# A two-layer hybrid attention step on one core: a new order of the attention parts, norm sums that add squares before the one-column product, and value products issued for two key tiles at a time

## The chip, the core and the metric

The kernel runs on one core of a Trainium2 chip. Its engines are TensorE (PE, with its weight loads shown apart as PEld), VectorE (DVE), ScalarE (ACT), GpSimd (POOL) and SyncE (SP), which issues nearly all transfers. The metric is the device time of one launch in microseconds; lower is better.

## What is computed

One inference step of a backbone of two layers (DEPTH = 2), in fp32, on 128 context tokens and 512 latent tokens of width 1024. Cut to one layer and to the latent tokens (the context tokens pass through the same layer with a conditioning vector of their own and attend to context alone):

```python
sh1, sc1, g1, sh2, sc2, g2 = jnp.split(jax.nn.silu(cvec) @ w_ada + b_ada, 6, axis=-1)
h = rmsnorm(x, norm1_g) * (1 + sc1) + sh1
da_q, da_k, da_v, sw_q, sw_k, sw_v, q_a, kv_a = jnp.split(h @ w_in, offs, axis=-1)
da_o  = diff_attention(q1, q2, [cache | k1], [cache | k2], dv, lam)     # 4 heads, softmax(1) - lam * softmax(2)
sw_o  = swa_latent_attention(q, k, v, cache_k, cache_v, sink)           # 8 heads, 2 key heads, window 128
mla_o = gqa_attention(q, [cache_k | k], [cache_v | v])                  # 4 heads, keys and values from a latent
mix = concat([rmsnorm(da_o, diff_subln_g) * (1 - lam_init), sw_o, mla_o])
x = x + g1 * (mix @ w_out)
h2 = rmsnorm(x, norm2_g) * (1 + sc2) + sh2
x = x + g2 * (square(relu(h2 @ w_up)) @ w_down)                         # 4096 hidden columns
```

`rmsnorm(x) = x * rsqrt(mean(x * x) + EPS) * g`; a last one stands behind the two layers. The keys and values of the context tokens are outputs too.

## The kernel before

**Data.** Activations are kept transposed: `xT` is [128, 8, 640], the eight 128-column chunks of the width on the partitions and the 640 tokens along the free axis. Tokens are handled in two halves, `HALVES = [(0, 256), (256, 640)]`, that is two and three tiles of 128 (`TILES`). A product in fp32 is made of three passes over split operands (`mm3`): high by high, high by low, low by high. So each weight block that arrives (`wr`) is split in `wh` (a rounding copy, on ACT or DVE) and `wl` (a subtraction, on DVE or GpSimd).

**Order.** Everything but the middle of the MLP is recorded as tasks of a planner (`Plan`): an engine or a choice of engines ("A" ACT, "V" DVE, "G" GpSimd, "P" PE), a modelled duration, what it reads and writes, which buffers of which ring it takes (`RINGS`: how many buffers each ring has), and a priority, lower first. `Plan.run` plays the tasks against the modelled durations and so fixes one order for each engine; the instructions are then emitted in that order, and an engine never leaves it. Transfers follow each other in SP's queue in the same way.

**Stages of a layer.** (1) Squares and sums for the first norm, its root, the modulated activations `h` (`emit_h`). (2) The input projection. (3) The attention: the sequence of parts `seq` in the table `KP`, one for each layer. A token `cN` is N conditionings (two chunks of a section of `w_ada`: a load, products `pa`, an `asb` copy, a transpose, `ada`; they supply shifts, scales and gates needed later, those of the next layer's first norm among them). `s0`, `s1` are quads (groups of two heads by two query tiles) of the windowed attention, `d0`, `d1` of the differential and `m0`, `m1` of the latent one. `D`, `V`, `M` prepare queries, keys and values, `wN` is part N of the output product. The place of a token gives the priority of its tasks; `lead`, `prep`, `tr` and `evict` shift kinds of them, and the other entries choose engines (`weights`, `caches`, `keys`, `da`, `out`, `scale`). (4) The output stage: last part of the output product, residual updates (`emit_resid`, a scaled addition to `xT` on DVE), sums for the second norm, its root for each half, `h2`, and the first up products of the MLP (`first_up`). (5) The big product stage of the MLP, in a list `blocks` of up ("u") and down ("d") products written out in order. (6) The last down products (`last_down`), with the sums for the next norm.

**The norm's sums** (`stat`): for each chunk and half, ACT squares `xT` into a buffer `sq` of ring "E" (four buffers), and PE multiplies each 128-token tile of it by a column of ones, which adds the 128 partitions; the eight chunks add up in PSUM (`st`). This happens at five places: at the start, in the output stage of either layer, between the layers, at the end. The root (`rstd`) is a chain of small steps on DVE (`rsq`), a broadcast copy `yb` and transposes on PE into `rb`. In the plan `emit_h` for the second half of the tokens stands `half` (in priority) behind that of the first, with `k` from 0 to 7 as the step of one chunk.

**A quad**: scores into PSUM (`sps`), row maximum on DVE, exponential on ACT (`quad`), the scaling of each row by one over its sum (`scale`, L981 on ACT, L983 on DVE), then for each key tile transposes into PSUM (`pt`, L1095), a copy `PT` to SBUF by ACT or DVE, and the value products (L1099): two heads side by side, 64 output columns of the array each, over up to 256 queries, added up over the key tiles in `O`. Ring "PT" has three buffers.

Of the kernel before, what the change touches and what calls it, by code (L numbers as in the profile page):

```python
# [15 lines left out]
ALU = mybir.AluOpType  # L16
# [11 lines left out]
HALVES = [(0, 256), (256, 640)]  # L28
# [14 lines left out]
N_CST = 900  # L43


RINGS = {"E": 4, "X": 5, "PT": 3, "B": 8, "h": 4, "mix": 3, "quad": 2, "QK": 4, "hs": 2, "wr": 3, "wh": 4, "wl": 4, "zin": 2, "sq4": 2,
         "stt": 10, "osb": 1, "Kc": 1, "ds": 2, "sm": 4, "rsq": 3, "Vsw": 1, "Vda": 1, "Vml": 1, "ckT": 1, "kz": 1,
         "s": 2, "t": 3, "o": 1, "z": 4, "T": 2, "ws": 2}

# [7 lines left out]
DMA0, DMAR = 2.0, 300e3  # L57
WINDOW = 3.413
N_PRE = 2

KP = [
    {"weights": ("A", "V"), "caches": ("A", "V"), "keys": ("AV", "V"), "da": ("AV", "V"), "out": ("AV", "V"),
     "scale": "AV", "lead": 5, "prep": 1000000.0, "tr": 1000000.0, "up": ("A", "V"), "up_prio": 3500000.0,
     "evict": 500000.0, "resid": (4, 4, 8, 8), "half": 0.5,
# [15 lines left out]
def tV(n):  # L82
    return 0.07 + n / 960
# [281 lines left out]
def tile_hybrid_step(ctx: ExitStack, tc: tile.TileContext, i, o):  # L365
    nc = tc.nc
    V, S, G, T = nc.vector, nc.scalar, nc.gpsimd, nc.tensor
# [22 lines left out]
    def add(*a, **k):  # L390
        return cur[0].add(*a, **k)
# [43 lines left out]
    def sl(t, table, key):  # L435
# [11 lines left out]
    ones = sl(cst, CST, "ones")  # L447
# [18 lines left out]
                    in1=sil[:, 2].rearrange("p (k s) -> p k s", s=2), op=ALU.mult)  # L466
# [162 lines left out]
    def open_stats(ring, after=()):  # L629
        if ring == "s":  # L630
            x = mk(ring, [P, 2, 512], F32, "st")
            add("V", 0.1, lambda: V.memset(x.t[:, :, 0:4], 0.0), alloc=[x], prio=0.0, after=after)
            return [(x, lambda a, b, hf=hf: x.t[:, hf, a:b]) for hf in range(2)]
# [3 lines left out]
        return [(x, lambda a, b, x=x: x.t[:, a:b]) for x in st]  # L637

    def stat(st, k, hf, prio):

        a, b = HALVES[hf]
        w = b - a
        n = TILES[hf][1] - TILES[hf][0]
        x, view = st[hf]
        sq = mk("E", [P, NT], F32, "sq")
        add("A", tA(w) + 0.05, lambda: S.activation(out=sq.t[:, 0:w], in_=xT[:, k, a:b], func=AF.Square),
            r=[("x", (k, hf))], alloc=[sq], prio=prio)

        def mm():
            for t in range(n):  # L650
                T.matmul(out=view(t, t + 1), lhsT=sq.t[:, t * P:(t + 1) * P], rhs=ones,  # L651
                         start=False, stop=(k == KD - 1), skip_group_check=True)

        add("P", 0.115 * n, mm, r=[sq], w=[(x, hf)], prio=min(prio, 0.9e6))
# [331 lines left out]
    def quad(l, kind, u, hd, vt, vcols, mix, kt_mix, pr_, hs, at):  # L986
# [9 lines left out]
        for y in range(2):  # L996
            for x in range(2):
                n = 2 * pr_ + y
                h = hd[x]
                q = slice(P + n * P, 2 * P + n * P)  # L1000
                st = mk("stt", [P, 8])
                e2 = mk("E", [P, NT], F32, "e2") if kind == "da" else None
                if kind == "sw":
                    a, tiles = SWT[n]
                    w = len(tiles) * P
                    we = w + 1
                else:
                    w = we = NT
                for j in range(2 if kind == "da" else 1):
# [20 lines left out]
                    else:  # L1030
# [54 lines left out]
        ns = len(slots)  # L1085
        O = mk("o", [P, 256], F32, "O")
        p_t = PAR["tr"] + at
        for z, (kt, have) in enumerate(slots):
            pt, PT = mk("t", [P, 2, 256], F32, "pt"), mk("PT", [P, 2, 256], F32, "PT")
            c, w = have[0] * P, len(have) * P  # L1090

            def tr(pt=pt, kt=kt, have=have):
                for x in range(2):
                    for y in have:
                        T.transpose(pt.t[:, x, y * P:(y + 1) * P], e_.t[:, x, y, pos[y][kt]:pos[y][kt] + P], ident)  # L1095

            def pv(z=z, kt=kt, c=c, w=w, PT=PT):
                for x in range(2):
                    T.matmul(out=O.t[64 * x:64 * x + 64, c:c + w], lhsT=vt.t[:, kt, vcols[x]:vcols[x] + 64],  # L1099
                             rhs=PT.t[:, x, c:c + w], start=(z == 0), stop=(z == ns - 1))  # L1100
# [477 lines left out]
    for l in range(DEPTH + 1):  # L1578
# [134 lines left out]
        with ExitStack() as es:  # L1713
# [108 lines left out]
            for b_, blk in enumerate(blocks):  # L1822
# [182 lines left out]
```

## Time and profile before

| | |
|---|---|
| time, three runs | 1755.74, 1760.19 and 1761.95 us; median 1760.19 |
| the profiled execution | 1761.53 us, of it 1759.8 us from the first instruction to the last (span) |
| PE | 1676.2 us busy (95%), 11335 products |
| DVE | 1242.9 us (71%) |
| ACT | 809.5 us (46%) |
| POOL | 199.5 us (11%) |
| transfers | 163.24 MB, 93 GB/s in the mean |

A row of a group reads: line, engine, operation, written and read buffers, partitions by elements and type, count, then busy us and mean ns of one, then the engine's idle time just before these instructions with what ended it. A row of a time table reads: window in us from the start, its length, then busy us and count of PE, PEld, DVE, ACT and POOL, the clock that TensorE was granted (1.00 is full), the share of the DMA engines and GB/s. A row of a timeline reads: start, duration, engine, line, operation, buffers, and in brackets the wait before it and what ended it. "x400" beside the norm's sums counts two passes of PE for each fp32 product of the code.

### The profile page before, as it was taken

The numbers are of one execution on the slowest core, as the hardware profiler recorded it, in microseconds if no ns is written. First come the engines' busy times: TensorE is split into PE (matmuls) and PEld (weight loads), VectorE is DVE, ScalarE is ACT, GpSimd is POOL, SyncE is SP. The second block draws the span as 40 slices with busy tenths as digits, with TensorE's granted clock in tenths as the row PEclk, the third lists the DMA queues.
The fourth block names the chain that finished last, engine by engine and source line by source line (L and its number), as shares of the span: only waits on it lengthen the run. The fifth ranks groups of instructions, "written<-read, shape, count | busy, mean of one in ns | idle before, by whom it ended". The sixth has DMA issues, their size and how long they took to land.

```text
span 1759.8 us, 29841 instructions
## 1 busy us (share of the span) xinstructions
PE 1676.2 (95%) x11335; PEld 1487.5 (85%) x11335; DVE 1242.9 (71%) x3229; ACT 809.5 (46%) x1798; POOL 199.5 (11%) x165
## 2 busy tenths in 40 slices
PE   7899999899899999999999999989889999999997
PEld 6687567568799999999998865857779999999997
DVE  3865778986868667766576767988577867766654
ACT  3532667774525333333254347777353433333321
POOL 0000001100013222212000000300001322212200
PEclk9999999999899999999999999999999999999999
DMA  9322553340122122222213244231111222222121
GB/s 314 102 84 87 200 165 96 108 139 25 61 70 87 61 87 82 97 85 77 89 52 98 88 135 137 90 108 56 36 61 50 71 93 76 96 88 70 61 73 61
DMA packets 67391, 163.24 MB, mean 93 GB/s; under 512 B 6896, under 2 KB 31280, under 8 KB 67248
## 3 DMA queue, kind: packets, MB, share of 16 engines
q1 hardware_dynamic: 67248, 161.34, 28.3%
q8 instruction: 90, 1.47, 0.3%
q14 instruction: 53, 0.43, 0.1%
HBM read 153.15 MB, written 8.16 MB: 92 GB/s over the span
## 4 chain that ended last, share of the span: by engine, by line
PE 79%; DVE 10%; ACT 4%; DMA 2%; issue 1%; POOL 1%; SPq 0%; DVEq 0%; ACTq 0%; POOLq 0%
PE pu L1853 18%; PE pu L543 8%; PE pu L542 8%; PE pu L544 8%; PE pt L1095 3%; PE O L1099 3%; PE po L542 3%; PE po L544 3%; PE pz L830 3%; PE pz L832 3%; PE po L543 3%; PE pz L831 3%; PE sps L1026 2%; PE st L651 2%; DMA zin<-zda 2%
## 5 line engine op out<-in xcount | busy, mean ns | idle before, releaser
L407 DVE TENSOR_TENSOR wl<-wr,wh 128x512 fp32r<-128x512 f32 (+2 forms) x290 | 287.0, 1010 | 62.0 <-ACT wh L414 37.4
L399 ACT ACTIVATE wh<-wr 128x512 fp32r<-128x512 f32 (+1 forms) x228 | 161.0, 736 | 282.6 <-PE pu L543 176.3
L542 PE MATMUL pu<-Gt,wh 128*128 128x384 f32 (+1 forms) x896 | 277.7, 310 | 5.1 <-DVE r L1449 5.1
L543 PE MATMUL pu<-Gt,wh 128*128 128x384 f32 (+1 forms) x896 | 277.6, 310 | 0.0
L544 PE MATMUL pu<-Gt,wl 128*128 128x384 f32 (+1 forms) x896 | 277.6, 310 | 0.0
L735 DVE SCALAR_TENSOR_TENSOR xT<-pu,ada,xT 128x128 f32<-128x128 f32 x336 | 134.8, 434 | 146.0 <-PE pu L544 145.7
L542 PEld LDWEIGHTS pu<-Gt,wh 128*128 128x128 f32 x896 | 170.6, 190 | 5.7 <-DVE r L1449 5.7
L543 PEld LDWEIGHTS pu<-Gt,wh 128*128 128x128 f32 x896 | 170.6, 190 | 0.0
L544 PEld LDWEIGHTS pu<-Gt,wl 128*128 128x128 f32 x896 | 170.5, 190 | 0.0
L1853 PE MATMUL pu<-Tl,wh 128*128 128x320 f32 x448 | 138.0, 308 | 0.0
L1853 PE MATMUL pu<-Th,wl 128*128 128x320 f32 x448 | 138.0, 308 | 0.0
L1853 PE MATMUL pu<-Th,wh 128*128 128x320 f32 x448 | 138.0, 308 | 0.0
L830 PE MATMUL pz<-wh,hh 128*128 128x512 f32 (+1 forms) x320 | 128.3, 401 | 2.1 <-DVE m L763 1.0
L831 PE MATMUL pz<-wl,hh 128*128 128x512 f32 (+1 forms) x320 | 123.4, 386 | 2.6 <-DVE wl L407 2.6
L735 DVE SCALAR_TENSOR_TENSOR xT<-po,ada,xT 128x128 f32<-128x128 f32 (+1 forms) x192 | 77.0, 434 | 66.3 <-PE po L544 65.2
L832 PE MATMUL pz<-wh,hl 128*128 128x512 f32 (+1 forms) x320 | 123.7, 386 | 0.1
L1048 DVE TENSOR_REDUCE stt<-sps 128x1 f32<-128x640 f32 (+2 forms) x160 | 116.1, 737 | 9.1 <-PE sps L1041 5.0
L1853 PE MATMUL pu<-hh,wh 128*128 128x320 f32 x336 | 104.2, 310 | 4.6 <-DVE r L1868 4.6
L1056 ACT ACTIVATE quad<-sps,stt 128x640 f32<-128x640 f32 (+2 forms) x128 | 91.2, 713 | 27.5 <-DVE stt L1048 26.9
L1853 PE MATMUL pu<-hh,wl 128*128 128x320 f32 x336 | 103.8, 309 | 0.0
L1853 PE MATMUL pu<-hl,wh 128*128 128x320 f32 x336 | 103.6, 308 | 0.0
L1427 POOL TENSOR_TENSOR xT<-xT,tm 128x256 f32<-128x256 f32 (+1 forms) x32 | 30.1, 941 | 619.8 <-ACT tm L1423 365.3
(313 smaller groups left out, 3930.7 us busy)
## 6 DMA issues: line engine op xcount, KB each, us to landing
wr<-in_w_ada SPq DMA_DIRECT2D x80, 512.0 KB, 3.8
wr<-in_w_up SPq DMA_DIRECT2D x64, 512.0 KB, 3.5
wr<-in_w_down SPq DMA_DIRECT2D x64, 512.0 KB, 3.5
wr<-in_w_in SPq DMA_DIRECT2D x24, 512.0 KB, 3.5
wr<-in_w_out SPq DMA_DIRECT2D x16, 512.0 KB, 4.5
wq<-in_w_ada SPq DMA_DIRECT2D x6, 1024.0 KB, 6.9
wr<-in_w_in SPq DMA_DIRECT2D x8, 416.0 KB, 3.4
xT<-in_xT SPq DMA_DIRECT2D x4, 640.0 KB, 7.1
```

The lines of the kernel that those rows point to most:

```text
L399: S.activation(out=out, in_=in_, func=AF.Copy)
L407: eng.tensor_tensor(out=out, in0=a, in1=b, op=ALU.subtract)
L542: T.matmul(out=out, lhsT=w[0], rhs=a[0], start=first, stop=False)
L543: T.matmul(out=out, lhsT=w[0], rhs=a[1], start=False, stop=False)
L544: T.matmul(out=out, lhsT=w[1], rhs=a[0], start=False, stop=last)
L735: V.scalar_tensor_tensor(out=xT[:, m, a:b], in0=po[:, a - a0:b - a0], scalar=ada[l][:, sec, m, s:s + 1], in1=xT[:, m, a:b], op0=ALU.mult, ...
L830: T.matmul(out=out, lhsT=h_at(h, "h", k, tk), rhs=wh[:, x], start=(k == 0), stop=False)
L831: T.matmul(out=out, lhsT=h_at(h, "h", k, tk), rhs=wl[:, x], start=False, stop=False)
L832: T.matmul(out=out, lhsT=h_at(h, "l", k, tk), rhs=wh[:, x], start=False, stop=(k == KD - 1))
L1048: add("V", tV(we) - 0.01, lambda st=st, j=j, view=view: V.tensor_reduce(out=st.t[:, j:j + 1], in_=view(), axis=AX.X if kind == "sw" else A ...
L1056: S.activation(out=out, in_=view(), func=AF.Exp, bias=st.t[:, j:j + 1], accum_out=st.t[:, 4 + j:5 + j])
L1853: T.matmul(out=out, lhsT=w_[:, k], rhs=a_[:, k], start=new and k == 0 and y == 0, stop=k == 3 and y == 2, skip_group_check=True)
```

## The change

Four things, in one edit.

1. `stat` adds the squares of chunks 0 to 6 on DVE into the first one's buffer, which stays taken for that time; PE multiplies this sum by ones when chunk 6 is in, and the square of chunk 7 by itself. So 10 one-column products at each of the five places, where there were 40.
2. `N_PV = 2`: in a quad the value products of two key tiles are one task, behind both copies `PT`; a last odd tile goes alone. Ring "PT" has four buffers.
3. `KP` has new entries for both layers: the sequence with conditionings one by one between the quads, other priorities (`lead`, `prep`, `tr`, `evict`, `half`) and other engines.
4. In the big product stage a down block covers both 128-column pieces (`mi`) of one half of the tokens, where it covered both halves of one piece. The products are the same.

```diff
-RINGS = {"E": 4, "X": 5, "PT": 3, ...
+RINGS = {"E": 4, "X": 5, "PT": 4, ...
...
+N_PV = 2
...
 KP = [
-    {"weights": ("A", "V"), "caches": ("A", "V"), "keys": ("AV", "V"), "da": ("AV", "V"), "out": ("AV", "V"),
-     "scale": "AV", "lead": 5, "prep": 1000000.0, "tr": 1000000.0, ...
-     "evict": 500000.0, "resid": (4, 4, 8, 8), "half": 0.5,
-     "seq": "c2 c1 c1 c2 s0 s0 s0 c2 c2 s0 c2 c1 w0 s1 c2 s1 D0 s1 s1 ..."
+    {"weights": ("A", "V"), "caches": ("AV", "V"), "keys": ("A", "V"), "da": ("AV", "V"), "out": ("AV", "V"), "scale": "AV",
+     "lead": 40, "prep": 1000000.0, "tr": 900000.0, ... "evict": 1000000.0,
+     "resid": (4, 4, 8, 8), "half": 3.0,
+     "seq": "c1 c1 c1 c1 s0 s0 c1 c1 s0 c1 c1 c1 c1 s0 s1 c1 s1 D0 s1 s1 c1 w0 ..."
...
-    {"weights": ("A", "V"), "caches": ("AV", "VG"), "keys": ("AV", "V"), "da": ("AV", "V"),
-     "out": ("AV", "V"), "scale": "AV", "lead": 30, "prep": 950000.0, "tr": 900000.0, ...
-     "split": "V", "evict": 999995.0, "resid": (4, 4, 8, 8), "half": 0.5, ...
+    {"weights": ("AV", "V"), "caches": ("A", "V"), "keys": ("A", "V"), "da": ("A", "V"), "out": ("AV", "V"), "scale": "A",
+     "lead": 30, "prep": 1000000.0, "tr": 900000.0, ... "evict": 1000000.0,
+     "resid": (4, 4, 8, 8), "half": 8.5, ...
...
 def stat(st, k, hf, prio):
-        x, view = st[hf]
+        x, view, part = st[hf]
         sq = mk("E", [P, NT], F32, "sq")
         add("A", tA(w) + 0.05, lambda: S.activation(out=sq.t[:, 0:w], in_=xT[:, k, a:b], func=AF.Square),
             r=[("x", (k, hf))], alloc=[sq], prio=prio)
+        if k == 0:
+            part.append(sq)
+        elif k < KD - 1:
+            acc = part[0]
+            add("V", tV(w), lambda: V.tensor_tensor(out=acc.t[:, 0:w], in0=acc.t[:, 0:w], in1=sq.t[:, 0:w], op=ALU.add),
+                r=[sq], w=[acc], prio=prio)
+        if k < KD - 2:
+            return
+        src = part[0] if k < KD - 1 else sq
 
         def mm():
             for t in range(n):
-                T.matmul(out=view(t, t + 1), lhsT=sq.t[:, t * P:(t + 1) * P], rhs=ones,
+                T.matmul(out=view(t, t + 1), lhsT=src.t[:, t * P:(t + 1) * P], rhs=ones,
                          start=False, stop=(k == KD - 1), skip_group_check=True)
...
 def quad(...):
-        for z, (kt, have) in enumerate(slots):
+        z0, pvs = 0, []
+        for kt, have in slots:
...
-            add("P", 0.255 * len(have), pv, r=[PT, (vt, kt)], ... prio=p_t, narrow=True)
+            pvs.append((kt, c, w, PT))
+            if len(pvs) < N_PV and kt != slots[-1][0]:
+                continue
...
+            add("P", 0.255 * sum(w // P for _, _, w, _ in pvs), pv,
+                r=[q for kt, _, _, PT in pvs for q in (PT, (vt, kt))], ... prio=p_t, narrow=True)
+            z0, pvs = z0 + len(pvs), []
...
-                        blocks.extend(("d", g, mc, mi, len(tiles)) for mi in range(2))
+                        blocks.extend(("d", g, mc, hf, len(tiles)) for hf in range(2))
...
-                    for hf in range(2):
-                        a0, b0 = HALVES[hf]
+                    for mi in range(2):
+                        m = mc * 2 + mi
+                        mm_ = slice(mi * P, (mi + 1) * P)
```

What the edit moves shows in the engines' orders. PE at the start: `st` are the norm's sums, `pa` the first conditionings (whose transposes write `pt`), `rb` the transposed root of a half. Before:

```order
L651 MATMUL st<-cst,sq 128x1 x37
L576 MATMUL pa<-wq,sc 32x128 x8
L651 MATMUL st<-cst,sq 128x1 x3
L581 MATMUL pt<-cst,asb 128x128
L576 MATMUL pa<-wq,sc 32x128 x8
L581 MATMUL pt<-cst,asb 128x128
L669 MATMUL rb<-cst,yb 128x128 x5
```

After:

```order
L663 MATMUL st<-cst,sq 128x1 x10
L578 MATMUL pa<-wq,sc 32x128 x16
L681 MATMUL rb<-cst,yb 128x128 x2
L583 MATMUL pt<-cst,asb 128x128 x2
L578 MATMUL pa<-wq,sc 32x128 x8
L681 MATMUL rb<-cst,yb 128x128 x3
```

The 40 products of the sums are 10, and the root's transposes of the first half (two) stand ahead of the last conditioning, those of the second half (three) behind it. PE in the first layer's windowed attention, from one quad's transposes (L1095) to the next part: `O` are value products of the latent tokens, `Oc` those of the context. Before:

```order
L1095 MATMUL pt<-cst,quad 128x128 x4
L1215 MATMUL Oc<-PTc,Vsw 64x128 x2
L1095 MATMUL pt<-cst,quad 128x128 x8
L1099 MATMUL O<-PT,Vsw 64x256 x2
L576 MATMUL pa<-wr,sc 32x256 x4
L1099 MATMUL O<-PT,Vsw 64x256 x2
L1265 MATMUL pt<-cst,sq_2625 128x128 x4
L1099 MATMUL O<-PT,Vsw 64x256 x2
L1099 MATMUL O<-PT,Vsw 64x128 x2
L1265 MATMUL pt<-cst,sq_2642 128x128 x4
```

After:

```order
L1108 MATMUL pt<-cst,quad 128x128 x8
L583 MATMUL pt<-cst,asb 128x128 x2
L1108 MATMUL pt<-cst,quad 128x128 x4
L578 MATMUL pa<-wr,sc 32x256 x4
L1122 MATMUL O<-PT,Vsw 64x256 x6
L1122 MATMUL O<-PT,Vsw 64x128 x2
L1285 MATMUL pt<-cst,sq_2333 128x128 x4
L1285 MATMUL pt<-cst,sq_2338 128x128 x4
```

The value products of a quad stood in four pieces between other work; the new order has those of two key tiles, and here of all four, next to each other, behind all the transposes. DVE in the second layer's output stage, where the residual updates of the second half of the tokens (128x384) meet the root and the `h2` work of the first half (128x256; `hs`, `hh`, `hl`). Before:

```order
L719 TENSOR_TENSOR hs<-xT,rb 128x256
L407 TENSOR_TENSOR hl_14617<-hs,hh_14615 128x256
L719 TENSOR_TENSOR hs<-xT,rb 128x256 x2
L585 TENSOR_REDUCE ada_93<-pt 128x4
L587 TENSOR_TENSOR ada_93<-ada_93,cols 128x4
L407 TENSOR_TENSOR hl_14617<-hs,hh_14615 128x256
L401 CAST hh_14615<-hs 128x256
L735 SCALAR_TENSOR_TENSOR xT<-po,ada_93,xT 128x384
L407 TENSOR_TENSOR hl_14617<-hs,hh_14615 128x256
L735 SCALAR_TENSOR_TENSOR xT<-po,ada_93,xT 128x384
```

After:

```order
L747 SCALAR_TENSOR_TENSOR xT<-po,ada_93,xT 128x384
L655 TENSOR_TENSOR sq<-sq 128x384
L747 SCALAR_TENSOR_TENSOR xT<-po,ada_93,xT 128x384
L655 TENSOR_TENSOR sq<-sq 128x384
L623 TENSOR_TENSOR rsq<-rsq 128x2
L747 SCALAR_TENSOR_TENSOR xT<-po,ada_93,xT 128x384
L655 TENSOR_TENSOR sq<-sq 128x384
L624 SCALAR_TENSOR_TENSOR rsq<-rsq 128x2
L409 TENSOR_TENSOR wl<-wr,wh 128x1024
L625 SCALAR_TENSOR_TENSOR rsq<-rsq 128x2
L613 TENSOR_SCALAR rsq<-st 128x3
```

The last updates of the second half stood within the `h2` work of the first half, behind its root; now they all stand ahead of the end of that root, each with an addition of squares (L655) behind it.

More of the change, by code (lines that the diff above doesn't have):

```diff
@@ L43 @@
 N_CST = 900
-RINGS = {"E": 4, "X": 5, "PT": 3, "B": 8, "h": 4, "mix": 3, "quad": 2, "QK": 4, "hs": 2, "wr": 3, "wh": 4, "wl": 4, "zin": 2, "sq4": 2,
+RINGS = {"E": 4, "X": 5, "PT": 4, "B": 8, "h": 4, "mix": 3, "quad": 2, "QK": 4, "hs": 2, "wr": 3, "wh": 4, "wl": 4, "zin": 2, "sq4": 2,
          "stt": 10, "osb": 1, "Kc": 1, "ds": 2, "sm": 4, "rsq": 3, "Vsw": 1, "Vda": 1, "Vml": 1, "ckT": 1, "kz": 1,
@@ L59 @@
 N_PRE = 2
+N_PV = 2
 KP = [
-    {"weights": ("A", "V"), "caches": ("A", "V"), "keys": ("AV", "V"), "da": ("AV", "V"), "out": ("AV", "V"),
-     "scale": "AV", "lead": 5, "prep": 1000000.0, "tr": 1000000.0, "up": ("A", "V"), "up_prio": 3500000.0,
-     "evict": 500000.0, "resid": (4, 4, 8, 8), "half": 0.5,
[4 rows of a table removed]
-     "up_prio": 3500000.0, "split": "V", "evict": 999995.0, "resid": (4, 4, 8, 8), "half": 0.5,
-     "seq": "s1 s0 c1 c2 s1 c1 s1 s1 c1 D0 c1 s0 c1 c1 c1 s0 s0 w1 c1 "
-            "w0 d0 c1 D1 V0 c1 c1 c1 d0 d1 M0 d1 c1 w2 m0 m0 M1 m1 m1"},
+    {"weights": ("A", "V"), "caches": ("AV", "V"), "keys": ("A", "V"), "da": ("AV", "V"), "out": ("AV", "V"), "scale": "AV",
+     "lead": 40, "prep": 1000000.0, "tr": 900000.0, "up": ("A", "V"), "up_prio": 3500000.0, "evict": 1000000.0,
+     "resid": (4, 4, 8, 8), "half": 3.0,
+     "seq": "c1 c1 c1 c1 s0 s0 c1 c1 s0 c1 c1 c1 c1 s0 s1 c1 s1 D0 s1 s1 c1 w0 "
+            "c1 w1 c1 d0 c1 c1 V0 c1 c1 c1 D1 c1 d1 d0 c1 d1 M0 c1 m0 m0 c1 w2 "
+            "M1 m1 m1"},
+    {"weights": ("AV", "V"), "caches": ("A", "V"), "keys": ("A", "V"), "da": ("A", "V"), "out": ("AV", "V"), "scale": "A",
+     "lead": 30, "prep": 1000000.0, "tr": 900000.0, "up": ("A", "V"), "up_prio": 3500000.0, "evict": 1000000.0,
+     "resid": (4, 4, 8, 8), "half": 8.5,
+     "seq": "c1 s0 s1 s1 c1 c1 c1 s1 s1 D0 c1 s0 c1 c1 c1 s0 w1 s0 w0 c1 c1 c1 "
+            "d0 V0 D1 d0 c1 c1 c1 c1 d1 M0 d1 m0 m0 M1 w2 m1 m1"},
 ]
@@ L632, in open_stats @@
             add("V", 0.1, lambda: V.memset(x.t[:, :, 0:4], 0.0), alloc=[x], prio=0.0, after=after)
-            return [(x, lambda a, b, hf=hf: x.t[:, hf, a:b]) for hf in range(2)]
+            return [(x, lambda a, b, hf=hf: x.t[:, hf, a:b], []) for hf in range(2)]
         st = [mk(ring, [P, 512], F32, "st") for _ in range(2)]
@@ L636, in open_stats @@
             add("V", 0.1, lambda x=x: V.memset(x.t[:, 0:4], 0.0), alloc=[x], prio=0.0, after=after)
-        return [(x, lambda a, b, x=x: x.t[:, a:b]) for x in st]
+        return [(x, lambda a, b, x=x: x.t[:, a:b], []) for x in st]
     def stat(st, k, hf, prio):
@@ L647, in stat @@
             r=[("x", (k, hf))], alloc=[sq], prio=prio)
+        if k == 0:
[7 more added lines that the diff above has]
+        src = part[0] if k < KD - 1 else sq
         def mm():
             for t in range(n):
[L651 removed]
+                T.matmul(out=view(t, t + 1), lhsT=src.t[:, t * P:(t + 1) * P], rhs=ones,
                          start=False, stop=(k == KD - 1), skip_group_check=True)
[L654 removed]
+        add("P", 0.115 * n, mm, r=[src], w=[(x, hf)], prio=min(prio, 0.9e6))
     def rstd(st, hf, rb, prio):
@@ L1095, in tr @@
                         T.transpose(pt.t[:, x, y * P:(y + 1) * P], e_.t[:, x, y, pos[y][kt]:pos[y][kt] + P], ident)
[L1097 to L1100, printed above, removed]
             add("P", 0.22 * len(have), tr, r=[(e_, (x, y)) for x in range(2) for y in have],
@@ L1106, in quad, with pv @@
                 r=[pt], alloc=[PT], prio=PAR["evict"] + at)
-            add("P", 0.255 * len(have), pv, r=[PT, (vt, kt)], w=[] if z == 0 else [O], alloc=[O] if z == 0 else [], prio=p_t,
-                narrow=True)
+            pvs.append((kt, c, w, PT))
+            if len(pvs) < N_PV and kt != slots[-1][0]:
+                continue
+            def pv(pvs=pvs, z0=z0, O=O):
+                for z, (kt, c, w, PT) in enumerate(pvs):
+                    for x in range(2):
+                        T.matmul(out=O.t[64 * x:64 * x + 64, c:c + w], lhsT=vt.t[:, kt, vcols[x]:vcols[x] + 64],
+                                 rhs=PT.t[:, x, c:c + w], start=(z0 + z == 0), stop=(z0 + z == ns - 1))
+            add("P", 0.255 * sum(w // P for _, _, w, _ in pvs), pv,
+                r=[q for kt, _, _, PT in pvs for q in (PT, (vt, kt))], w=[] if z0 == 0 else [O],
+                alloc=[O] if z0 == 0 else [], prio=p_t, narrow=True)
+            z0, pvs = z0 + len(pvs), []
         c0 = P + pr_ * 256
@@ L1826, in tile_hybrid_step @@
                 if kind == "d":
-                    g, mc, mi = f, q, x
-                    m = mc * 2 + mi
-                    mm_ = slice(mi * P, (mi + 1) * P)
+                    g, mc, hf = f, q, x
+                    a0, b0 = HALVES[hf]
                     whv, wlv = (z.rearrange("p (k n) -> p k n", k=4) for z in (wh, wl))
-                    for hf in range(2):
-                        a0, b0 = HALVES[hf]
+                    for mi in range(2):
+                        m = mc * 2 + mi
+                        mm_ = slice(mi * P, (mi + 1) * P)
                         pu = bank()
```

3 rows, old and new, of the table KP are left out of this document.

## Prediction

> **What bounds the kernel now.** I read the page first: span, busy time by engine, the chain that ended last by engine.
>
> ```profile
> span 1759.8 us, 29841 instructions
> PE 1676.2 (95%) x11335; PEld 1487.5 (85%) x11335; DVE 1242.9 (71%) x3229; ACT 809.5 (46%) x1798; POOL 199.5 (11%) x165
> PE 79%; DVE 10%; ACT 4%; DMA 2%; issue 1%; POOL 1%; SPq 0%; DVEq 0%; ACTq 0%; POOLq 0%
> ```
>
> PE ends the program: work taken off it counts unless another engine is about as full in that stage. So I cut the span where PE goes from one stage to the next. The rows are the start, the first attention, the output stage (output product, norm, first up products), the big product stage, the last down products, the second attention, the second output stage; the columns are busy us of PE, PEld, DVE, ACT, POOL, then the granted clock.
>
> ```profile
> 0.00:34.00 34.00, 24.38 (x153) 21.25 (x154) 9.24 (x47) 12.89 (x28) 0.20 (x4) 1.00 0.96 327
> 173.00:419.00 246.00, 231.04 (x1811) 159.93 (x1811) 194.91 (x547) 172.76 (x428) 17.46 (x24) 0.99 0.42 132
> 419.00:524.00 105.00, 93.74 (x609) 89.59 (x609) 72.61 (x165) 41.13 (x80) 8.04 (x6) 0.93 0.15 51
> 524.00:868.00 344.00, 341.99 (x2334) 341.46 (x2333) 239.04 (x418) 124.36 (x232) 74.44 (x50) 1.00 0.25 85
> 868.00:904.00 36.00, 36.00 (x267) 36.00 (x265) 22.61 (x66) 17.40 (x39) 0.00 (x0) 1.00 0.13 38
> 1026.00:1267.00 241.00, 225.03 (x1707) 163.87 (x1705) 198.15 (x543) 165.56 (x416) 17.12 (x25) 0.98 0.32 100
> 1267.00:1367.00 100.00, 88.75 (x569) 84.57 (x568) 70.81 (x159) 39.72 (x76) 8.07 (x6) 0.93 0.16 53
> ```
>
> The big product stage (524 to 868) and the last down products have no room but less PE work. The attentions are full on PE (94%) with DVE at 79 and 82%: there a PE saving may turn into a wait. The output stages are where PE is least busy.
>
> **Part 1: squares summed first.** 200 one-column products become 50; the trace shows each as two passes (400 in all), so 300 passes go. 60 DVE additions come: 30 of 256 columns, 30 of 384. Their price from the same form on DVE, and that of a pass from a place where nothing waits, the last down products:
>
> ```profile
> L651 PE MATMUL st<-cst,sq 128*128 128x1 f32 x400 | 57.0, 261 | 8.0 <-ACT sq L646 8.0
> L407 DVE TENSOR_TENSOR hl<-hs,hh 128x256 fp32r<-128x256 f32 x16 | 6.5, 420 | 0.0
> L407 DVE TENSOR_TENSOR hl<-hs,hh 128x384 fp32r<-128x384 f32 x8 | 4.4, 551 | 0.0
> 879.89 0.50 PE L651 MATMUL st<-cst,sq 128*128 128x1 f32 x4
> 881.65 0.28 PE L544 MATMUL po<-Gt,wl 128*128 128x256 f32 x1
> 881.77 0.50 PE L651 MATMUL st<-cst,sq 128*128 128x1 f32 x4
> 881.97 0.61 DVE L735 SCALAR_TENSOR_TENSOR xT<-po,ada,xT 128x128 f32<-128x128 f32 x2 [1.27 <-PE po L544]
> ```
>
> One round (12 products, 4 passes) takes 881.77 - 879.89 = 1.88 us; a product starts 0.12 us after the last (881.77 - 881.65), so the passes take 1.88 - 12 x 0.12 = 0.44, or 0.11 each. 300 x 0.11 = 33 us of PE work at full clock, 6.6 in each of five places; the additions are 30 x 0.42 + 30 x 0.55 = 29 us of DVE. What a place yields depends on who waits.
>
> Last down products, both layers: DVE idles 1.27 us per round and now adds 0.42, so it stays ahead. Between the layers 6.5. At the end DVE also writes the result, so 5.5; bounds 4 and 6.6 each.
>
> Start: these passes run at half speed and hold up the squares.
>
> ```profile
> 7.58 15.95 PE L651 MATMUL st<-cst,sq 128*128 128x1 f32 x74 [7.58 <-ACT sq L646]
> 9.97 0.52 ACT L646 ACTIVATE sq<-xT 128x384 f32<-128x384 f32 x1 [0.77 <-PE st L651]
> 23.56 0.16 DVE L611 TENSOR_SCALAR rsq<-st 128x2 f32<-128x2 f32 x1 [19.55 <-PE st L651]
> 66.77 0.50 PE L830 MATMUL pz<-wh,hh 128*128 128x512 f32 x1 [0.92 <-DVE hh L401]
> 69.84 0.80 PE L831 MATMUL pz<-wl,hh 128*128 128x512 f32 x1 [2.57 <-DVE wl L407]
> ```
>
> 15.95 / 74 = 0.215 us a pass; ACT waits for the buffers they read, and DVE idles 19.55 us until the sum is there. After: two of four buffers are pinned as sums, so a round of both halves is two squares and two additions in turn, at least 0.42 + 0.55 = 0.97 on DVE and about 1.15 with the hand-overs. Eight from 7.1 end near 16; the first half's seven products of two passes then take 3 us at most at 0.215, partly beside the last squares, so the root starts near 17.5, not 23.56. DVE then makes h until the waits at 66.77 and 69.84, both for DVE, so the gain runs through the projection: 6. Bounds 3.5 (the loads, busy 96% here, end last) and 7.
>
> The Trainium skill speaks against that term. TensorE: Matmul & The Clock Gate, "Part 1: The HAM clock gate (the "warmup" mystery)", says that the half clock is released after about 3.4 us of sustained products. By that rule the passes after 11 us would take 0.11, the old chain would end near 18 and the start would gain nothing: 1725 in place of the 1719 below. The row shows 0.215 held for 16 us, so the measurement decides.
>
> The first output stage in pieces, and two forms of DVE there (a split of a weight block, a residual update):
>
> ```profile
> 418.00:425.00 7.00, 7.00 (x57) 6.48 (x57) 2.86 (x9) 1.94 (x5) 0.00 (x0) 1.00 0.00 0
> 425.00:432.00 7.00, 4.70 (x32) 4.03 (x31) 3.28 (x10) 0.42 (x1) 0.00 (x0) 1.00 0.01 2
> 432.00:440.00 8.00, 8.00 (x56) 8.00 (x56) 4.67 (x14) 2.95 (x6) 0.00 (x0) 1.00 0.00 0
> 440.00:447.00 7.00, 7.00 (x52) 7.00 (x51) 4.50 (x14) 3.20 (x6) 0.00 (x0) 1.00 0.23 75
> 447.00:455.00 8.00, 7.71 (x61) 5.91 (x61) 6.98 (x23) 6.92 (x19) 0.00 (x0) 1.00 0.38 133
> 455.00:463.00 8.00, 8.00 (x69) 8.00 (x68) 7.98 (x20) 3.02 (x5) 0.00 (x0) 1.00 0.39 131
> 463.00:474.00 11.00, 4.86 (x19) 3.51 (x18) 8.31 (x23) 6.54 (x15) 0.00 (x0) 0.73 0.01 2
> 474.00:495.00 21.00, 18.46 (x97) 18.14 (x97) 17.62 (x25) 10.71 (x19) 0.00 (x0) 0.90 0.07 24
> ...
> L407 DVE TENSOR_TENSOR wl<-wr,wh 128x1024 fp32r<-128x1024 f32 x112 | 144.3, 1292 | 51.7 <-ACT wh L414 34.1 <-ACT wh L399 17.4
> L735 DVE SCALAR_TENSOR_TENSOR xT<-po,ada,xT 128x384 f32<-128x384 f32 x64 | 39.4, 616 | 39.5 <-PE po L544 39.0
> ```
>
> Output stages up to the norm's first half: DVE is busy 15.3 of 29 us there (418 to 447, four rows), PE 26.7. After, PE loses the 6.6, but DVE gains 5.8 of additions, two late residual updates (0.62 each) and one or two splits of weights (1.3 each) that stood behind: about 24. So DVE is the bound, some 24 for 29: I take 4 in each layer, 8 in all; bounds +3 (the additions delay the updates) and -13 (all of PE's).
>
> **Part 2: the first up products.** From 447 to 495 DVE is busy 40.9 of 48 us; PE stands idle 6 of 11 us around 468, for the second half's root, and falls to half clock. In the new order the second half's updates all stand ahead of the first half's h, and its transposed root comes after 63 (first layer) and 27 (second) of the 96 up products, not after them. DVE's work here shrinks by what moved ahead, 1.2 + 1.3 to 2.6 + some root steps of 0.16, to about 37, plus hand-overs 39; from 46 (448 to the first down product at 494.3) that is 7 a layer, 14 in all. Bounds 4 (DVE waits anyway) and 18 (PE's idle and half clock of both layers gone).
>
> **Part 3: value products by twos, four buffers.** The order has 49 and 43 visits to these narrow products in the attentions before, 28 and 28 after: 36 fewer for the same 288 products.
>
> ```profile
> 414.34 0.65 PE L1099 MATMUL O<-PT,Vml 128*64 128x256 f32 x4
> 414.92 0.66 PE L1095 MATMUL pt<-cst,quad 128*128 128x128 f32 x4
> 341.19 1.45 PE O L1099 x12
> 363.89 1.01 PE O L1099 x8
> ...
> L399 ACT ACTIVATE PT<-pt 128x512 f32<-128x512 f32 x82 | 47.7, 596 | 29.2 <-PE pt L1095 26.8 <-PE O L1099 1.6
> L401 DVE COPY PT<-pt 128x512 f32<-128x512 f32 x46 | 31.1, 686 | 8.3 <-PE pt L1095 8.1
> ```
>
> One tile pair takes 0.58 (414.92 - 414.34), two 1.01, three 1.45: 0.435 each and 0.145 a visit. 36 x 0.145 = 5.2; a little more may lie in the transpose ahead, so 6. Bounds 0 (PE waits for the second copy instead) and 9.
>
> **Part 4: the new sequence and engines.** No product is added. Over both layers 25 row scalings go from ACT to DVE, most of them in the second attention, and some weight casts with them:
>
> ```profile
> L981 ACT ACTIVATE quad<-quad,stt 128x640 f32<-128x640 f32 x15 | 12.3, 825 | 2.9 <-DVE stt L1078 2.9
> L983 DVE TENSOR_SCALAR quad<-quad,stt 128x640 f32<-128x640 f32 x17 | 9.3, 550 | 0.4
> ```
>
> At these prices and those of the other forms DVE gets some 12 us more in the second attention, where it is busy 198 of 241, and ACT 15 less. I charge 4: a third, since a scaling itself is shorter (0.55 for 0.83). Bounds -2 and +12. Conditionings one by one, earlier key preparation and changed priorities only reorder: the attentions' PE idle time, 15 and 16 us, may shrink or grow; 0, bounds -10 and +12. The SP queue keeps its 417 instructions, with w_ada loads spread between zin reads; a read behind a load that waits for a buffer would show in this last term. The swapped down blocks in the big stage do the same 24 + 24 products, DVE at 239 of 344 covers either order: 0; uncovered, it would be one update, 0.6, a block.
>
> **Sum.** -6 - 6.5 - 5.5 - 8 - 14 - 6 + 4 + 0 = -42. The profiled execution took 1761.5, so 1719.5; the median of the three runs, 1760.2, is 1.3 lower, so 1718.
>
> **Rivals.** (a) The attentions give it back, but no more: parts 2 and 3 shrink to their low bounds, the reorder costs 8: -6 - 12 - 4 - 4 + 8 = -18 to -25: 1735 to 1742. For it: DVE is already 80% full there. Against: ACT gets lighter by 17.
> (b) More: PE's idle in the attentions falls by 10 and each term reaches near its bound, about -65: 1696 or less.
> (c) Slower: merged value products wait for the second copy. Some 96 groups each need two copies (0.60 on ACT, 0.69 on DVE); where PE has nothing else to run, a group costs one, 0.65. It takes back the 42 at 65 groups and, at 80, ends near 1770. Against: the row at 414 shows PE going from transposes to value products without idle time, and a fourth buffer lets the next transposes run.
> (d) No change: DVE's 29 us of additions return what PE gave, at every place. Against: DVE's idle 1.27 us a round, and 19.55 at the start.
> (e) The output stages fall to half clock with the passes gone: some 17 us of products twice would cost 34, 1753. At 67% PE busy (425 to 432) the clock stayed 1.00, at 44% (463 to 474) it fell; I expect 75%.
>
> **Chances.** Forecast (1702 to 1733) 0.55; (a) 0.17; (b) 0.14; (c) 0.07; (d) 0.04; (e) 0.03. The range leaves out (c), (d), (e) and the far ends of (a) and (b): 1696 to 1746. Within 0.3% (5 us, about what a measurement here can tell from no change): (d), 0.04. Slower: (c), 0.07. Faster: the rest, 0.89.
>
> **What would show it.** Right: 100 passes at that line in place of 400; the root's first step near 17.5; no PE idle stretch of over 4 us behind the first up products, granted clock near 1.00 in the second; some 56 visits of value products; DVE over 200 us in the second attention, PE idle there still 13 to 18. Wrong: PE waiting at value products for copies, or DVE over 90% with PE idle above 25 in an attention.

## The result, and the profile after

The changed kernel takes 1699.2 us (median; 1696.9 to 1702.1), the kernel before 1759.9 in the same runs: ratio 0.966 (95% interval 0.964 to 0.968). That is 61 us less where 42 were forecast. Three parts of the page after: span, busy time, chain that ended last.

```profile
span 1697.4 us, 29299 instructions
PE 1612.8 (95%) x11035; PEld 1444.5 (85%) x11035; DVE 1279.2 (75%) x3317; ACT 788.3 (46%) x1771; POOL 202.7 (12%) x164
PE 76%; DVE 14%; ACT 4%; DMA 2%; issue 2%; POOL 1%; DVEq 0%; ACTq 0%; SPq 0%; POOLq 0%
```

PE is as full as before (95%) and still ends the program, with 63 us less of busy time (1676.2 - 1612.8); DVE got 36 us more, and the chain runs over it for 14% in place of 10. By stages, in the columns of the prediction's table: start, first attention, output stage with the first down blocks, the rest of the big product stage, last down products, second projection, second attention, second output stage with its first down blocks, the rest of the second big product stage, end.

```profile
0.00:25.00 25.00, 9.89 (x94) 8.08 (x95) 13.96 (x57) 12.10 (x28) 0.20 (x4) 1.00 0.99 333
160.00:395.00 235.00, 223.68 (x1827) 164.99 (x1828) 195.91 (x555) 168.19 (x424) 17.86 (x24) 0.99 0.44 138
395.00:490.00 95.00, 83.08 (x532) 80.29 (x531) 77.45 (x175) 40.13 (x80) 8.51 (x6) 0.91 0.16 56
490.00:834.00 344.00, 342.03 (x2332) 341.50 (x2331) 241.28 (x417) 124.07 (x231) 74.06 (x50) 1.00 0.26 85
834.00:863.00 29.00, 29.00 (x202) 28.97 (x201) 23.48 (x72) 15.43 (x33) 0.00 (x0) 1.00 0.11 33
863.00:991.00 128.00, 123.75 (x606) 104.15 (x605) 86.48 (x387) 48.74 (x121) 0.00 (x0) 1.00 0.27 83
991.00:1218.00 227.00, 213.43 (x1672) 158.16 (x1673) 202.41 (x557) 150.62 (x392) 19.38 (x24) 1.00 0.33 106
1218.00:1316.00 98.00, 88.81 (x585) 85.99 (x584) 81.69 (x183) 44.51 (x87) 8.78 (x7) 0.93 0.18 60
1316.00:1654.00 338.00, 335.63 (x2289) 335.11 (x2288) 235.22 (x411) 121.00 (x226) 73.87 (x50) 1.00 0.23 79
1654.00:1697.00 43.00, 32.12 (x220) 31.28 (x218) 28.45 (x82) 8.61 (x17) 0.00 (x0) 0.89 0.18 61
```

The first attention is 11 us shorter (246 to 235), the second 14 (241 to 227), the first output stage with its down blocks 10 (105 to 95); the rest of the first big stage is as it was (344). In the second layer the cut falls elsewhere, so the two stages are taken together: 436 us, where they were 445 before (1267 to 1712). For all that follows, PE's span is cut in three: idle time (span less busy), what half clock cost (half of PE's busy time in the stretches with a granted clock of 0.5), and the rest, its work at full clock (the passes of the start count there). In us:

| kernel | time | ratio to before (95%) | work | half clock | idle |
|---|---|---|---|---|---|
| before | 1759.9 | | 1655.7 | 20.4 | 83.6 |
| the full change | 1699.2 | 0.966 (0.964-0.968) | 1598.1 | 14.7 | 84.6 |
| sums alone | 1721.0 | 0.978 (0.977-0.980) | 1610.2 | 22.7 | 89.3 |
| twos alone (with the fourth buffer) | 1739.6 | 0.988 (0.985-0.991) | 1644.2 | 14.9 | 80.0 |
| table alone | 1767.4 | 1.005 (1.003-1.006) | 1652.8 | 26.2 | 87.1 |
| sums and twos, old table | 1706.7 | 0.971 (0.969-0.973) | 1603.7 | 10.8 | 89.3 |
| sums and table, no twos | 1730.8 | 0.985 (0.983-0.987) | 1610.4 | 23.3 | 95.4 |
| fourth buffer alone | 1751.5 | 0.997 (0.996-0.998) | 1648.7 | 28.2 | 76.0 |

(Work, half clock and idle time are of the profiled execution, so they add up to its span; the times are medians.) The work column is the plain part: singly -45.5, -11.5 and -2.9, together -59.9, and the full change has -57.6. That they meet so closely is in part luck: sums and twos have -52.0 for -57.0, and sums, table and fourth buffer -45.3 for -55.4. Idle time and half clock don't add: each order has its own.

### The profile page after: what moved, and what is told of

It is laid out like the page before. It is cut to its first block, busy times and chain, and to the rows that moved or that the text cites. A ratio compares the mean times of both kernels' runs of the same rounds, so it can differ in the third digit from the quotient of the medians.

```text
span 1697.4 us, 29299 instructions
## 1 busy us (share of the span) xinstructions
PE 1612.8 (95%) x11035; PEld 1444.5 (85%) x11035; DVE 1279.2 (75%) x3317; ACT 788.3 (46%) x1771; POOL 202.7 (12%) x164
## 4 chain that ended last, share of the span: by engine, by line
PE 76%; DVE 14%; ACT 4%; DMA 2%; issue 2%; POOL 1%; DVEq 0%; ACTq 0%; SPq 0%; POOLq 0%
PE pu L1873 19%; PE pu L546 8%; PE pu L545 8%; PE pu L544 8%; PE po L544 3%; PE pt L1108 3%; PE O L1122 3%; PE po L546 3%; PE po L545 3%; PE pz L842 3%; PE pz L844 3%; PE pz L843 3%; PE sps L1046 1%; PE pa L578 1%; DVE wl L409 1%
## 5 line engine op out<-in xcount | busy, mean ns | idle before, releaser
L409 DVE TENSOR_TENSOR wl<-wr,wh 128x512 fp32r<-128x512 f32 (+2 forms) x290 | 293.8, 1034 | 58.4 <-ACT wh L416 30.3
L409 POOL TENSOR_TENSOR wr<-wr 128x512 f32<-128x512 f32 x28 | 38.3, 1366 | 479.2 <-DMA wr<-in_w_up 326.0
```

The source lines that it names most:

```text
L409: eng.tensor_tensor(out=out, in0=a, in1=b, op=ALU.subtract)
```

## The experiments

**1. Part 1 alone**: `stat` and its sums as in the change, the rest as before.

> The kernel before with part 1 alone (squares summed on DVE ahead of the one-column product; 50 products for 200). Theory 'the parts add up': the start and first projection gain the 12.8 us that the full change showed there, the boundary between the layers 2 to 7, the end 5, and the two output stages, whose h2 order stays as it was, 4 to 8 each: 28 to 41 us, 1719 to 1732. Rival 'DVE gives it back in the output stages': there nothing is gained or some is lost, so only the start, the boundary and the end count, 15 to 20 us: 1740 to 1745. The time in the attentions should not move by more than 3 us by either.

Measured 1721.0, 38 us less: the parts theory (28 to 41). By stages: start -8.6, first projection -0.5, last down products -7.2 with +4.1 in the projection behind them, end -4.7, attention and output stage together -14.0 and -8.2. The rival is out. The first layer's output stage gained more than the 4 to 8 us of the theory: from the last value product to the first down block this kernel takes 62.6 us for 75.5 (first layer) and 64.8 for 70.6 (second). In PE's order the sum of the second half now stands ahead of the first up products, and the waits for the second half's root and `h2` behind them are gone (0.3 us of them is left in the second layer).

**2. Part 3 alone.**

```diff
-RINGS = {... "PT": 3 ...    +RINGS = {... "PT": 4 ...
+N_PV = 2     (and the value products of quad as in the change)
```

> The kernel before with part 3 alone (value products of two key tiles in one task, four PT buffers); the order has 69 visits to the narrow products for 107. The two attentions together were 25.6 us shorter after the full change. Theory 'visits cost more than 0.145 us': most of that comes back here, 15 to 25 us, 1735 to 1745. Rival 'the sequence did it': 38 visits at 0.145 are 5.5 us, 1752 to 1756. A second rival, the waits for the second copy: PE idle time in the attentions rises above the 31 us of before, time at 1760 or above.

1739.6, 19 us less (the spans differ by 20.6): work -11.5, half clock -5.5, idle -3.6. For 38 visits (107 to 69 in the order, with those of the context tokens) the work alone is 0.30 a visit, twice the forecast's 0.145. A reason shows in the trace of before, in the transposes around the product that the prediction priced:

```profile
410.85 0.60 PE L1095 MATMUL pt<-cst,quad 128*128 128x128 f32 x4
411.20 0.36 PE L542 MATMUL po<-mix,wh 128*128 128x256 f32 x1
...
413.77 0.64 PE L1095 MATMUL pt<-cst,quad 128*128 128x128 f32 x4
```

Four transposes between wide products take 0.35 (411.20 - 410.85). Four with a 64-column product behind them take 0.57: the next row, at 414.34, is in the prediction. So between transposes a visit costs 0.145 in the product and 0.22 in the transposes, 0.37; over all such places of the attentions at full clock, a transpose (L1095) right ahead of a visit takes 0.203, one behind it 0.165, where 0.109 is usual (36, 46 and 326 of them, medians): 0.145 + 0.094 + 0.056 = 0.295. The Trainium skill has a mechanism: TensorEngine Tiling (Array Packing), "Key Properties", says that changing the tiling mode drains TensorE. The rows agree with it, since the delay stands on both sides of the switch, and give a price that the page does not. So a visit costs more than its product; what it costs in a whole attention is less sure, for the work column gives 0.18 a visit between sums alone and sums with twos (37 visits), 0.37 when the twos are undone in the full change (33), and 0.58 for the fourth buffer alone (12).

**3. Part 4 alone**: the new `KP`, nothing else.

> The kernel before with part 4 alone (the new table: sequence, priorities, engines). Theory 'the sequence did it': the attentions get 15 to 20 us shorter and the first up products 5 to 14 (the second half's root comes earlier): 1728 to 1740. Rival 'visits cost more': the attentions gain under 5 us; with the up products' gain 1742 to 1755. Second rival 'the table fits only the rest of the change': the attentions get longer, 1760 or more.

1767.4, slower by 8: the second rival. Attention and output stage of the first layer grew by 10.3 us, and half clock there by 11.2. PE's rows of this kernel at one such place, and its time around it:

```profile
246.08 0.83 PE L1266 MATMUL pt<-cst,sq 128*128 128x128 f32 x4 [2.13 <-DVE sq L408]
...
240.00:246.00 6.00, 3.65 (x38) 1.95 (x36) 4.99 (x13) 2.90 (x7) 0.00 (x0) 1.00 0.67 194
246.00:250.00 4.00, 3.92 (x22) 2.77 (x22) 2.67 (x6) 2.96 (x9) 0.00 (x0) 0.57 0.54 173
250.00:256.50 6.50, 3.92 (x40) 1.84 (x38) 5.72 (x17) 2.07 (x6) 0.00 (x0) 1.00 0.82 263
256.50:263.40 6.90, 6.39 (x33) 4.00 (x34) 4.92 (x12) 3.44 (x8) 0.00 (x0) 0.51 0.56 180
```

Where PE works 3.65 of 6 us, with a wait of 2.13 for DVE, the next 3.4 us run at half clock, and so on after the thin stretch behind it: PE looks full there (3.92 of 4.00) while it runs at half speed.

**4. The old order of the down blocks** in the full change.

```diff
-blocks.extend(("d", g, mc, hf, ...) for hf in range(2))    +blocks.extend(("d", g, mc, mi, ...) for mi in range(2))
```

> The changed kernel with the old order of the down blocks in the big product stage (both halves of one 128-column piece in a block). Forecast's theory: the swap is worth nothing, 1696 to 1702 as the full change. Rival: it decides how long PE waits at the first down block (5.7 us in the first layer, 4.3 in the second): with the old order PE waits for the second half's hidden units there too, some 2 to 4 us more in each layer, 1703 to 1708; or it was the swap that lengthened these waits (2.5 us each before), and undoing it gains 3 to 6: 1693 to 1696.

1698.2, ratio 0.966: no change, as forecast. Both rivals are out; PE's waits at the first down block don't come from the swap.

**5 and 6. The full change without the table, and without the twos** (`N_PV` undone, four buffers kept).

> The changed kernel with the old table: parts 1 and 3 (and the down blocks) without part 4. Alone, the sums gave 38.0 us, the twos 19.4, the table lost 8.4, of which its trace shows 14.4 us of half clock in the first attention. Theory 'the parts add up, and the table's loss was the clock': sums and twos give 57, 1700 to 1704, so the table is worth 1 to 5 us inside the full change. Rival 'the table needs the others and carries the rest of the gain': without it the time is 1708 or more. Second rival 'the table costs 8 here too': 1690 to 1693.

> The changed kernel with one task for each key tile's value products (N_PV undone, four PT buffers kept); 105 visits for 72. From the instructions around a visit in the trace of before (the product itself 0.145 more than its neighbours, the transpose ahead of it 0.21 for 0.11, the one behind it 0.165 for 0.11) a visit costs 0.30 us: 33 visits are 10 us, and with as much idle time and half clock as the twos alone removed (8 us) 1709 to 1717. Rival, the forecast's 0.145: 1703 to 1705. Second rival, the clock: without the twos the table's first attention falls to half clock as it did alone, 10 us and more on top: 1720 to 1730.

Without the table 1706.7: between the two bounds given, so the table is worth 7.5 us inside the change. Without the twos 1730.8: the second rival's time, and a little more. Of the mechanism that it named, the trace shows a third: half clock in the first attention costs 5.0 us for 1.7, not 10 on top. The table's sign hangs on the twos: on top of the sums it costs 9.8 (1721.0 to 1730.8), and that with the fourth buffer, which alone gains 6.4 (experiment 8); on top of sums and twos it gives 7.5. The rows of the value products of the windowed attention, without the twos and in the full change:

```profile
L1111 PE MATMUL O<-PT,Vsw 128*64 128x256 f32 x192 | 27.7, 400 | 2.5 <-ACT PT L401 2.4
...
L1122 PE MATMUL O<-PT,Vsw 128*64 128x256 f32 x192 | 25.8, 391 | 0.0
```

One wait is seen: with this table and single tasks PE waits 2.5 us for the copies, with the twos not at all. It is a small part of the 31.6 us between the two kernels (work 12.3, half clock 8.6, idle 10.8 by their traces); the rest of the idle time is spread over many short waits, and no run takes it apart.

**7. By threes**, with five buffers (`N_PV = 3`, `"PT": 5`).

> The changed kernel with the value products of three key tiles in one task and five PT buffers; 60 visits for 72. Theory 'a visit costs 0.30 us': 3.6 us, 1694 to 1697. Rival 'the third copy is waited for': PE idle time in the attentions rises above the 25 us of the full change by 4 or more, 1699 to 1706.

1717.9 (ratio 0.977, 0.975 to 0.980): a loss of 19 us, more than the rival's. PE idles more in the attentions, as the rival said (36.2 us for 25.3), but not where it said: there are 60 visits and no wait at the value products. Scores, for one, wait longer for ACT's exponentials in the first attention (5.1 us for 3.1). Over the whole program idle time is 9.2 us higher, 4.5 more go to half clock, and the work is 4.6 higher, though fewer visits should lower it by 3.6. Tasks and buffers changed together here; which of them did it is open.

**8. The fourth buffer alone.**

> The kernel before with the fourth PT buffer alone, value products one key tile at a time as before; 95 visits for 107 in the order. Both halves of part 3 together gave 19.4 us (11.5 of it PE work, 5.5 half clock, 3.6 idle time). Theory 'the grouping did it, at 0.29 us a visit': 12 visits are 3.5 us, with a share of the rest 1752 to 1757. Rival 'the buffer did it': 1738 to 1746, the grouping adding little. Second rival: as in other orders the half clock decides; more than 5 us of it on top of before's 20, 1762 or more.

1751.5, 6.4 us less (ratio 0.997), just under the grouping theory's 1752 to 1757. Its trace is of the slowest of twelve executions (1754.6); by it work -7.0, idle -7.6, and 7.8 taken back by half clock. So by the medians the buffer alone is a third of part 3 and the grouping the rest. The work fell by twice what 12 visits explain (3.6); why is open.

**9. The split of the first down blocks early** in the full change.

```diff
-load_split(i["w_down"][l, 0, mc], 1024, 3.5e6 + 4 + mc, 4)
+load_split(i["w_down"][l, 0, mc], 1024, 0.4e6 + 400 + mc, 4, load_prio=3.5e6 + 4 + mc)
```

> The changed kernel with the splits of the first two down weight blocks (wh, wl) planned ahead of the last hidden units of the second half of the tokens. In the full change PE waits 5.7 us (first layer) and 4.3 us (second) at the first down block, in the first layer for this split, since DVE does eight steps for the second half's hidden units before it. Theory 'DVE's queue is the wait': PE starts on the first half's hidden units 3 to 4 us earlier in each layer, and waits again for the second half's within 1 us: 1692 to 1696. Rival 'DVE is full there anyway': the second half's units come as much later, and PE waits for them at the next block: 1698 to 1700.

The place in the full change, PE and DVE (first layer), and PE in the second:

```profile
460.53 0.58 PE L546 MATMUL pu<-Gt,wl 128*128 128x256 f32 x1 [5.66 <-DVE wl L409]
...
455.52 1.95 DVE L1469 SCALAR_TENSOR_TENSOR r<-pu,r 128x384 f32<-128x384 f32 x4
457.38 1.95 DVE L409 TENSOR_TENSOR Gt<-r,Gt 128x384 fp32r<-128x384 f32 x4
459.25 4.62 DVE L409 TENSOR_TENSOR wl<-wr,wh 128x1024 fp32r<-128x1024 f32 x4
...
1279.42 0.55 PE L544 MATMUL pu<-Gt,wh 128*128 128x256 f32 x1 [4.31 <-DVE r L1469]
```

PE wants the split `wl` at 454.9, and DVE has eight steps for the second half's hidden units first. With the split early this wait is 1.93 us, the big stage of the first layer 3.7 shorter; 1696.4 in all, 2.8 less than the full change, just above the theory's range, and no more than the two intervals leave open. In the second layer the rival holds: that layer begins 7.3 us earlier (856.4 for 863.6), its first down product only 3.5 (1275.89 for 1279.42), since PE waits longer there for the last hidden units (6.6 us in place of 4.3).

**10. Filler** in the same place: 40 products that nobody reads.

> The changed kernel with 40 extra products of 256 columns (0.107 us each at full clock, 4.3 us) ahead of the first down block of the first layer, where PE waits 5.7 us; their result is never read. In the full change the granted clock is half from 458.4 to 465.2 us of the profile, which costs 2.4 us of PE work there. Theory 'PE's idle time sets off the half clock': the spell is gone, the big product stage 1.5 to 3 us shorter, 1696 to 1698 and 377 to 378.5 us for that stage instead of 380.0. Rival 'the spell comes from something else': it stays, 380 us. Second rival 'the extra products end late': the stage gets longer than 380.

The time around the place, first in the full change, then with filler:

```profile
454.50:460.00 5.50, 0.36 (x3) 0.16 (x1) 5.50 (x10) 5.49 (x10) 0.00 (x0) 0.86 0.00 0
460.00:466.00 6.00, 5.47 (x26) 5.47 (x27) 4.86 (x8) 0.00 (x0) 0.00 (x0) 0.56 0.66 199
...
451.50:456.70 5.20, 5.20 (x45) 5.20 (x44) 5.20 (x10) 5.20 (x11) 0.00 (x0) 1.00 0.01 3
456.70:466.00 9.30, 8.43 (x60) 8.22 (x59) 7.20 (x12) 1.79 (x3) 1.85 (x2) 1.00 0.66 220
```

The half clock is gone, and the stage is 1.9 us shorter (378.1), though the 40 products took 4.8 us, 0.12 each: at this place idle time of PE sets the half clock off. The program's time did not move (1699.5). In the profiles the second layer, whose orders on PE, DVE and ACT are the same in both kernels, begins 4.5 us earlier, but this time takes 3.4 us more up to its first down block and 3.0 more in its big stage, with half clock of 5.2 us for 2.0 and of 4.9 for 2.4.

**11. The second layer's scalings planned for either engine** (`"scale": "AV"`).

> The changed kernel with the row scalings of the second layer planned for ACT or DVE by choice, as before. In the full change all 48 of that attention run on DVE (the trace shows none on ACT), 20 more than before, at 0.44 us, while the table's entry names ACT alone, so that the plan counts them there. Theory, the forecast's: DVE is charged for it, 2 to 6 us come back in the second attention, 1693 to 1697. Rival 'DVE at 202 of 227 us hides them': within 2 us of the full change, 1697 to 1701. Second rival 'any other order of this attention is worse': 1703 or more.

In the full change, DVE's scalings in the second attention:

```profile
L995 DVE TENSOR_SCALAR quad<-quad,stt 128x640 f32<-128x640 f32 x16 | 8.6, 546 | 0.1
L995 DVE TENSOR_SCALAR quad<-quad,stt 128x512 f32<-128x512 f32 x16 | 7.7, 481 | 0.2
L995 DVE TENSOR_SCALAR quad<-quad,stt 128x384 f32<-128x384 f32 x16 | 7.4, 460 | 0.1
```

All 48 run on DVE though the table says ACT: `soft_scale` falls back to DVE where the plan has one engine to choose from, so 23.7 us of DVE's work stand in the plan on the wrong engine. Planned rightly, 19 of them run on ACT, and the time is 1703.3 (ratio 0.969, 0.967 to 0.971), 4 us more, not less: the second rival's figure, though the intervals touch. So taking these 19 off DVE brought nothing back of what the forecast charged. Whether DVE hides them or the changed order costs what they gain, this run does not tell.

**12. A better mix**: the full change with the early split and the old table for the second layer.

> The changed kernel with the old table for the second layer and the early split of the first down blocks' weights. The traces with and without the table (sums and twos in both) put its worth in the first layer's attention and output at 9.4 us and in the second's at -0.3, with 2.2 lost in the second big product stage. Theory 'a layer's table acts on that layer alone': 2.5 us better than the early split with both tables, 1692 to 1696. Rival: the table of the second layer is needed for its half clock (3.6 us with the old one, 2.0 with the new), no gain, 1697 to 1702.

1692.6 (1692.2 to 1696.2; ratio 0.964, 0.962 to 0.965), 6.6 us less than the full change and the fastest kernel here. The theory's range held. By stages, against the full change, the big stages are 4.4 and 0.8 us shorter and the second projection 0.9, while the second layer's attention and output stage are 3.5 longer (half clock 7.0 there for 2.0). So by the trace the gain is that of the early split; that the old table suits the second layer better is not shown. The trace is of the slowest of five executions (1696.2) and accounts for 3.0 of the 6.6 us; the 3.8 us that the medians give beyond the early split alone stay open, and those two intervals overlap.

## Why the prediction was right, and where it was not

The range (1696 to 1746), the sign and the order of size held. The products of the sums were worth what they were taken to be (57.0 us of PE before, 15.4 after, for 33 forecast at full clock and some 6 more for the start's half speed), PE stayed the bound, and the additions on DVE were mostly hidden. But the sum was short by 20 of 62 us: the time lies below the forecast's own band (1702 to 1733, chance 0.55), and the range held it because it took in the near end of rival (b). By the prediction's own terms, with the spans' differences (-62.4 in all):

- **Start and first projection, -6: measured -12.8.** The root began at 15.53, not at 17.5, and the passes again ran at half speed, 0.22 us each (20 in 4.43):

```profile
13.62 4.43 PE L663 MATMUL st<-cst,sq 128*128 128x1 f32 x20 [13.62 <-DVE sq L655]
...
15.53 0.16 DVE L613 TENSOR_SCALAR rsq<-st 128x2 f32<-128x2 f32 x1 [1.15 <-PE st L663]
```

  This is the start's 8.8, of which the sums alone gave 8.6; the other 4.0 lie in the first projection, where the table alone also gained 5.1. The bound of 7 had left the table's part out; the loads, which would have meant 3.5, did not end last (PE's last wait ahead of the projection, 1.48 us, is for a copy by ACT).
- **Between the layers, -6.5: measured -2.2.** The last down products gained 7.2, and the second projection gave 5.0 back. The step that failed is "so it stays ahead": DVE does stay ahead of the sums, but the work behind them, on DVE and on ACT, is not ready when PE comes to the projection earlier.

```profile
877.52 0.49 PE L842 MATMUL pz<-wh,hh 128*128 128x512 f32 x1 [1.07 <-ACT hh L401]
883.61 0.44 PE L880 MATMUL pt<-cst,stk 128*128 128x128 f32 x2 [1.10 <-DVE stk L409]
```

  PE idles 4.1 us in that projection, 0.8 before; the sums alone lengthen it by 4.1, too. The prediction had put this wait at nothing.
- **End, -5.5: measured -5.0.**
- **Output stages and first up products, -8 and -14; value products, -6; table, +4 and 0: together -24, measured -42.5** (attention and output -27.1 and -22.9, given back at the first down blocks +6.5 and +1.0). Three steps failed. The price of a visit was taken from the product alone, 0.145, where the rows around it show 0.30; the twos with their buffer gave 19.7 here alone, for the 6 forecast. The gain of part 2 (14) was put on the new order, but the sums alone give 22.2 here, for the 8 that the prediction had for them in the output stages: the second half's root moves ahead with them already. Its waits (2.8 and 2.1 us) are gone, but in the first layer the second half's sum is waited for instead (3.51 at 417.33; the root that starts behind it has three tiles) and the first down block's split (5.66):

```profile
417.33 0.91 PE L663 MATMUL st<-cst,sq 128*128 128x1 f32 x4 [3.51 <-DVE sq L655]
...
419.99 0.16 DVE L613 TENSOR_SCALAR rsq<-st 128x3 f32<-128x3 f32 x1 [2.11 <-PE st L663]
```

  The granted clock of the output stage is no better (0.91 and 0.93 for 0.93): "no PE idle stretch of over 4 us behind the first up products" was wrong, and the first layer's stage got shorter by PE's work alone (idle time 11.9 of 95 us, 11.3 of 105 before). And the table was charged 4 whatever stands beside it: it cost 8.4 alone and gave 7.5 inside the change.
- **The signs to look for**: 100 passes, as said; DVE 202 us in the second attention and PE idle 13.6 there, as said (13 to 18); 56 visits of the latent tokens' value products and no wait at them, as said.

Rival (b), each term near its bound and less idle time in the attentions (15 and 16 us before, 11 and 14 after), comes closest to what happened. (c), value products that wait for the second copy, is not seen in the full change, nor by threes.

## What to carry to other kernels

Price a switch of mode from the instructions on both sides of it, not from the one that switches. Where one engine is 95% full, work taken off it adds up part by part, here within 3 us for the whole change and within 5 to 10 for two combinations of its parts, while idle time and half clock belong to an order as a whole: a table of priorities searched with one grain of tasks can lose with another, so it is to be tried together with what it was made for. Behind a stage that gets shorter, look for what its helper engine still has to do: here eight steps stood ahead of the one split that PE wanted.

## What the runs showed of the hardware

- Stretches of half clock ahead of the program's end last 3.4, 6.8 or 10.2 us, once 17.1 (in the fourth buffer alone), multiples of 3.41, and start behind stretches in which PE is thinly used: 3.65 of 6 us with a single wait of 2.13 was enough, and 40 idle-time products made one vanish. Cut into windows of 3.413 us on the grid of the clock's records (from the first record on, without the last 15 us), the 14 traces have 53 windows at full clock with PE busy under 48%; half clock follows 52 of them. It follows 43 of 315 with PE busy 48 to 78%, and none of 6315 above. The Trainium skill, TensorE: Matmul & The Clock Gate, "Part 1: The HAM clock gate (the "warmup" mystery)", puts the fall after an idle window of about 3.4 us; the length agrees, but no wait of that length was needed.
- Where such stretches fall changes with what came before: the same order of the second layer lost 2.4 us to half clock in one kernel's big stage and 4.9 in another's, where that layer began 4.5 us earlier. One and the same kernel moves as well: twelve executions of the fourth buffer alone spread over 5.6 us, the slowest with a granted clock of 0.978, the fastest with 0.983. Differences under some 4 us between single profiles of two orders can be this alone.
